# Two routers: half-tile logits behind the next half's products, ranking rounds between halves, and low halves behind the first gather

## The chip, the core and the metric

The kernel runs on one core of a Trainium2 chip. A core has five instruction queues that run in order and beside each other: TensorE (PE, matrix products into PSUM; its weight loads are listed as PEld), VectorE (DVE, elementwise work and searches), ScalarE (ACT, functions and copies), GpSimd (POOL, slow elementwise work and indirect DMAs) and SyncE (SP, which only starts DMAs here). They wait for each other by semaphores. The metric is the time of one execution on the device in microseconds, as the median of several runs.

## What is computed

Two layers of a diffusion backbone over 1024 latent and 256 context tokens of width 1024. Layer 0 mixes tokens with a bidirectional state-space scan (SSD), layer 1 with attention. After each mixer stands an expert-choice mixture of 16 experts: every expert picks its best tokens by a softmax over the experts.

```python
x = x + g1l * o_lat
x = x + g2l * moe_ec(rmsnorm(x, norm2_w[i]) * (1.0 + sc2l) + sh2l, ...)
...
def moe_ec(h, router_w, w1, w3, w2):
    logits = jnp.einsum('btd,de->bte', h, router_w)
    aff = jax.nn.softmax(logits, axis=-1)
    gate, idx = lax.top_k(jnp.swapaxes(aff, 1, 2), cap)   # cap = 2 * T // 16
    xg = h[bidx, idx]
    a = jnp.einsum('becd,edf->becf', xg, w1)
    g = jnp.einsum('becd,edf->becf', xg, w3)
    y = jnp.einsum('becf,efd->becd', jax.nn.silu(a) * g, w2)
    return jnp.zeros_like(h).at[bidx, idx].add(y * gate[..., None])
```

For 1024 latent tokens each expert takes 128, for 256 context tokens 32. Context tokens are only routed in layer 0.

## The kernel before

Tokens come in tiles of 128: ten in layer 0 (two of context, numbered 0 and 1, and eight of latents, 2 to 9, which go first), eight of latents in layer 1, numbered 0 to 7 here. Products in 32 bits are made of three passes: both operands are split into a high part (a copy by ScalarE, L48 and L722) and a low part (a subtraction on VectorE or GpSimd, L49, L723 and L725), and L54 to L56 multiply high by high, high by low and low by high.

**The output projection.** After each mixer a loop over tiles multiplies by the output weights, in two halves of 512 columns: 48 products a half in layer 0 (`ssd_out`, 16 blocks of rows in three passes), 24 in layer 1 (end of `attn`, 8 blocks). The products of a half are evaluated on VectorE: scaling by the gate (L626 in layer 0, L1254 in layer 1), adding the residual (L628, L1255), which gives `x1`. PSUM has two buffers for the first half (`o_ps0`) and one for the second.

**The router.** `Router.half` follows at once. It multiplies the half by a row of factors (L1341, into `u`, whose tiles are named h2), squares it on ScalarE with a sum (L1343), and `project` transposes the half on TensorE (L1318), copies it (L1320) and multiplies it by the router's weights into one PSUM bank (L1324). After the second half `Router.tile` makes the normalising factor (L1351, L159, L160), brings the logits into place (`logits`: L1329, L1331, L1332), writes them (L1355), finishes the normalised row (L1356) and starts two stores, the row to `h2` (L1359) and `x1` to `xs` (L1360), on SP, for the last tile on POOL.

**The ranking.** Tokens are ranked in parts: the first five latent tiles, the last three, and in layer 0 the two context tiles. `affinities` makes the softmax of a part and transposes it to one row per expert (L1368 to L1379). `rank` then finds the best 128 (32 for context) in rounds of eight, each with three searches on VectorE over the part's 640, 384 or 256 columns: MAX8 (L1390), FIND_INDEX8 (L1391), MATCH_REPLACE8 (L1393, not in the last round). `finish` merges the two latent rankings (L1403 to L1407), transposes the merged indices and gates on TensorE (L1409, L1410) and copies them (L1413, L1414). In layer 0 the ranking of the first part is called after the last latent tile and that of the second part ahead of the last context half's router; in layer 1 both are called after the loop.

**The first expert.** In `moe`, GpSimd gathers an expert's rows with an indirect DMA (L764); they are transposed and split, and `product` runs over four pieces of weights (`kp`), splitting each with GpSimd taking the last 128 (layer 0) or 256 (layer 1) of 1024 columns (L723) and VectorE the others (L725). In layer 1, GpSimd takes all columns of the first three pieces of the very first product. The split weights have three buffers.

**What sets the order.** The text is not the order in an engine's queue. A planner at compile time simulates the engines and gives each engine, when it comes free, the earliest instruction of the text that is ready, and one further down when that isn't. So an instruction can stand well before or behind its place in the text, and a place higher up in the text works as a priority. `issue_after(ins)` makes what is inside stand behind `ins` on that engine's queue, without waiting for its end.

Of the kernel before, what the change touches and what calls it, by code (L numbers as in the profile page):

```python
# [9 lines left out]
F32 = mybir.dt.float32  # L10
# [30 lines left out]
class Net:  # L41
# [534 lines left out]
    def ssd_out(self):  # L576
# [6 lines left out]
        with tc.tile_pool(name="op", bufs=2) as op:  # L583
# [3 lines left out]
            rt = Router(self, 0, op, pp, rk, [(NCT, NCT + 5), (NCT + 5, NT), (0, NCT)])  # L587
            for t in chain(range(NCT, NT), range(NCT)):
# [85 lines left out]
    def moe(self, i, ctx):  # L674
# [8 lines left out]
        with tc.tile_pool(name="mo", bufs=1) as mp, \  # L683
# [15 lines left out]
            def product(m, e, xl, xc, done=None):  # L699
# [16 lines left out]
                for kp in range(4):  # L716
                    n = D - (D if i and m + e == 0 and kp < 3 else share)
# [5 lines left out]
                    nc.gpsimd.tensor_tensor(w[1][:, :, n:], raw[:, :, n:], w[0][:, :, n:].bitcast(F32), op=OP.subtract)  # L723
                    if n:
                        nc.vector.tensor_tensor(w[1][:, :, :n], raw[:, :, :n], w[0][:, :, :n].bitcast(F32), op=OP.subtract)  # L725
# [150 lines left out]
            x = turn(gather(0))  # L876
# [82 lines left out]
    def attn(self):  # L959
# [273 lines left out]
        with tc.tile_pool(name="ao", bufs=2) as op:  # L1233
# [8 lines left out]
            rt.stream(0)  # L1242
            for t in range(NL):
                oh = self.hl_tile()
                self.split(q32[t].rearrange("p (j l) -> p j l", l=P), oh[0], oh[1], nc.gpsimd)
# [3 lines left out]
                for h in range(2):  # L1249
                    ps = pp.tile([P, 512], F32, name=f"o_ps{h}", bufs=2 - h)  # L1250
                    hs = slice(512 * h, 512 * h + 512)
                    for k in range(KT):
                        self.mm3(ps, [o[:, k] for o in oh], [w[:, k] for w in wo[h]], k == 0, k == KT - 1)
                    nc.vector.tensor_tensor(x1[:, hs], ps, gb[:, hs], op=OP.mult)  # L1254
                    nc.vector.tensor_tensor(x1[:, hs], x1[:, hs], xt[:, hs], op=OP.add)  # L1255
# [7 lines left out]
        first = rt.rank(0, af)  # L1263
# [21 lines left out]
class Router:  # L1285
# [48 lines left out]
    def half(self, x1, h):  # L1334

        nc, op = self.net.nc, self.op
# [9 lines left out]
    def tile(self, t, x1):  # L1346
# [10 lines left out]

        eng = nc.gpsimd if t + 1 == self.parts[-1][1] else nc.sync
        eng.dma_start(net.tile_of(net.h2d, t), self.u)  # L1359
        eng.dma_start(net.tile_of(net.xs, t), x1)  # L1360
# [21 lines left out]
    def rank(self, k, af, cap=CAPL):  # L1382

        net, nc, rp = self.net, self.net.nc, self.rk
        val = rp.tile([16, cap], F32, name=f"val{k}")
        idx = rp.tile([16, cap], U32, name=f"idx{k}")
        idf = rp.tile([16, cap], F32, name=f"idf{k}")
        for r8 in range(cap // 8):
            sl = slice(8 * r8, 8 * r8 + 8)
            nc.vector.max(val[:, sl], af)  # L1390
            nc.vector.max_index(idx[:, sl], val[:, sl], af)  # L1391
            if r8 + 1 < cap // 8:
# [76 lines left out]
```

## Time and profile before

| | us |
|---|---|
| median of three runs (3915.23 to 3926.81) | 3923.66 |
| the profiled execution, as timed | 3926.47 |
| its span, first to last instruction | 3924.7 |
| layer 0: output projection and router, to the first gathered rows | 1248 to 1530 |
| layer 0: experts | 1530 to 2360 |
| layer 1: attention | 2360 to 3083 |
| layer 1: output projection and router, to the first gathered rows | 3083 to 3286 |
| layer 1: experts and output | 3286 to 3924 |

The page of the profile gives busy time of each engine and the span in 40 slices of 98 us, busy shares in tenths:

```profile
PE 3570.0 (91%) x21153; PEld 2686.2 (68%) x21153; DVE 2620.5 (67%) x3749; ACT 2027.9 (52%) x3325; POOL 1814.0 (46%) x1402
...
PE   5999999888899997999999998899999874999997
...
DVE  4767777666633466666666655556656477999988
```

Slices 13 to 16 (1177 to 1570 us) hold layer 0's projection and slices 32 to 34 (3042 to 3336 us) layer 1's; the 4 in TensorE's row is the slice from 3238 to 3336. Other views used below are the waits (which engine waited for whom, us in total, number, longest), the timeline (start, duration, engine, line, operation, tiles, and in brackets the idle time before it and who ended it), the groups by line (count, busy us, mean ns) and busy time in stretches of the span.

### The profile page before, as it was taken

Reading aid. Unit: us, or ns where it says so; the run is one execution under the profiler, and the core shown is the slowest. Engines: PE = TensorE matmul, PEld = TensorE weight load, DVE = VectorE, ACT = ScalarE, POOL = GpSimd, SP = SyncE. Lnnn points to the kernel's source line nnn. Section 1 sums busy time; section 2 is a strip of 40 time slices with the busy share of each in tenths; the row PEclk is TensorE's granted clock in tenths of the full one; section 3 lists DMA queues with packets and bytes.
Section 4 is the critical chain, followed back from the end, with each engine's and each line's share of the span. In section 5 each row is a group of like instructions: output and inputs, shape, how many; then the busy total and the mean of one; then the engine's idle time right before and its main releaser. Section 6 shows DMA issues by size and latency. Waiting matters only on the chain.

```text
span 3924.7 us, 56652 instructions
## 1 busy us (share of the span) xinstructions
PE 3570.0 (91%) x21153; PEld 2686.2 (68%) x21153; DVE 2620.5 (67%) x3749; ACT 2027.9 (52%) x3325; POOL 1814.0 (46%) x1402
## 2 busy tenths in 40 slices
PE   5999999888899997999999998899999874999997
PEld 3767677777787775667666767677777653777765
DVE  4767777666633466666666655556656477999988
ACT  4544444544333223545555545477777433777665
POOL 1356545554543223566666652221111123777786
PEclk7999999999999998999999999999999987999999
DMA  4333332222444335889888863100000345999994
GB/s 171 103 103 127 115 96 77 76 76 74 143 142 144 126 115 183 325 313 330 313 319 307 285 236 92 38 15 1 1 1 12 129 142 212 386 376 376 350 338 172
DMA packets 296355, 681.08 MB, mean 174 GB/s; under 512 B 24192, under 2 KB 150000, under 8 KB 289936
## 3 DMA queue, kind: packets, MB, share of 16 engines
q1 hardware_dynamic: 269520, 615.50, 43.7%
q0 software_dynamic: 12720, 39.33, 4.1%
q10 hardware_dynamic: 13840, 22.63, 1.8%
q8 instruction: 167, 2.74, 0.3%
q14 instruction: 108, 0.88, 0.1%
HBM read 611.95 MB, written 62.82 MB: 172 GB/s over the span
## 4 chain that ended last, share of the span: by engine, by line
PE 54%; DVE 17%; POOL 9%; issue 9%; DMA 7%; ACT 4%; ACTq 0%; SPq 0%; POOLq 0%; DVEq 0%
DVE m_w L725 6%; PE pv L1171 5%; PE acc L54 4%; PE acc L56 4%; PE acc L55 4%; PE S L1137 4%; PE a_tr L1158 4%; PE cacc L696 4%; POOL m_w L723 3%; PE in_ps L55 3%; PE in_ps L54 3%; PE in_ps L56 3%; POOL Eb L422 2%; DMA m_raw<-in_moe_w_dram 2%; DMA Eb<-fd 2%
## 5 line engine op out<-in xcount | busy, mean ns | idle before, releaser
L725 DVE TENSOR_TENSOR m_w<-m_raw,m_w 128x1792 fp32r<-128x1792 f32 (+1 forms) x381 | 887.9, 2352 | 249.3 <-ACT m_w L722 247.1
L723 POOL TENSOR_TENSOR m_w<-m_raw,m_w 128x256 fp32r<-128x256 f32 (+1 forms) x384 | 816.1, 2149 | 387.9 <-ACT m_w L722 385.0
L722 ACT ACTIVATE m_w<-m_raw 128x2048 fp32r<-128x2048 f32 x384 | 732.8, 1916 | 483.2 <-DMA m_raw<-in_moe_w_dram 276.9
L54 PE MATMUL in_ps<-hh,w 128*128 128x512 f32 (+1 forms) x1152 | 427.6, 371 | 10.3 <-DVE th L499 10.3
L55 PE MATMUL acc<-m_w,xl 128*128 128x512 f32 x1024 | 406.9, 397 | 23.3 <-DVE m_w L725 12.5
L55 PE MATMUL in_ps<-hl,w 128*128 128x512 f32 (+1 forms) x1152 | 427.3, 371 | 0.0
L56 PE MATMUL in_ps<-hh,w 128*128 128x512 f32 (+1 forms) x1152 | 425.5, 369 | 0.0
L54 PE MATMUL acc<-m_w,xl 128*128 128x512 f32 x1024 | 405.6, 402 | 2.0 <-ACT xl L48 1.9
L56 PE MATMUL acc<-m_w,xl 128*128 128x512 f32 x1024 | 401.3, 392 | 0.0
L427 ACT ACTIVATE Eb<-Eb,ebias 128x128 f32<-128x128 f32 x640 | 202.2, 391 | 249.7 <-POOL Eb L422 249.5
L1141 DVE TENSOR_REDUCE mx<-S 128x1 f32<-128x1024 f32 x128 | 155.7, 1217 | 185.0 <-PE S L1137 184.9
L54 PEld LDWEIGHTS in_ps<-hh,w 128*128 128x128 f32 x1152 | 222.8, 193 | 52.8 <-issue 14.3
L55 PEld LDWEIGHTS acc<-m_w,xl 128*128 128x128 f32 x1024 | 193.2, 189 | 82.9 <-DVE m_w L725 26.9
L55 PEld LDWEIGHTS in_ps<-hl,w 128*128 128x128 f32 x1152 | 222.9, 193 | 39.1 <-issue 13.5
L1188 POOL TENSOR_TENSOR q<-s 64x128 f32<-64x128 f32 x128 | 57.5, 449 | 407.3 <-DVE mx L1146 339.5
L56 PEld LDWEIGHTS in_ps<-hh,w 128*128 128x128 f32 x1152 | 222.6, 193 | 31.7 <-issue 5.5
L54 PEld LDWEIGHTS acc<-m_w,xl 128*128 128x128 f32 x1024 | 193.0, 189 | 67.1 <-issue 14.4
L328 POOL TENSOR_TENSOR w<-w_raw,w 128x512 fp32r<-128x512 f32 x96 | 149.9, 1581 | 186.6 <-ACT w L325 181.3
L56 PEld LDWEIGHTS acc<-m_w,xl 128*128 128x128 f32 x1024 | 193.5, 189 | 38.1 <-DVE xl L49 0.2
L55 PE MATMUL acc<-m_w,gT 128*128 128x512 f32 x512 | 204.1, 399 | 6.6 <-DVE m_w L725 4.0
L54 PE MATMUL acc<-m_w,gT 128*128 128x512 f32 x512 | 202.2, 401 | 1.5 <-ACT gT L48 1.5
L56 PE MATMUL acc<-m_w,gT 128*128 128x512 f32 x512 | 202.3, 396 | 0.1
(385 smaller groups left out, 7724.7 us busy)
## 6 DMA issues: line engine op xcount, KB each, us to landing
m_raw<-in_moe_w_dram SPq DMA_DIRECT2D x384, 1024.0 KB
adw<-in_ada_w_dram SPq DMA_DIRECT2D x48, 1024.0 KB
Eb<-fd SPq DMA_DIRECT2D x80, 512.0 KB
w_raw<-in_ssd_in_w_dram SPq DMA_DIRECT2D x48, 512.0 KB
ydd<-yd SPq DMA_DIRECT2D x80, 128.0 KB
yt_raw<-yzd SPq DMA_DIRECT2D x40, 256.0 KB
xs<-x SPq DMA_DIRECT2D x16, 512.0 KB
h<-h SPq DMA_DIRECT2D x16, 512.0 KB
```

The source lines that it names most:

```text
L54: mm(out, lhs[0], rhs[0], start=start, stop=False)
L55: mm(out, lhs[0], rhs[1], start=False, stop=False)
L56: mm(out, lhs[1], rhs[0], start=False, stop=stop)
L427: nc.scalar.activation(Eb[:, d, hh, cc], Eb[:, d, hh, cc], AF.Exp, bias=bias[:, c0 + cc, k:k + 1])
L696: nc.tensor.matmul(acc[32 * q:32 * q + 32], xc[:, k], raw[:, k % 2, 256 * q:256 * q + 256], start=(k == 0), stop=(k == KT - 1))
L722: nc.scalar.activation(w[0], raw, AF.Copy)
L723: nc.gpsimd.tensor_tensor(w[1][:, :, n:], raw[:, :, n:], w[0][:, :, n:].bitcast(F32), op=OP.subtract)
L725: nc.vector.tensor_tensor(w[1][:, :, :n], raw[:, :, :n], w[0][:, :, :n].bitcast(F32), op=OP.subtract)
L1137: nc.tensor.matmul(o, qTs[self.qt][:, 2 * self.hp + hh], kT[k][:, self.kv, 512 * b:512 * b + n], start=(k == 0), stop=(k == 1))
L1141: nc.vector.tensor_reduce(self.mx[:, 0:1], S[hh], axis=AX.X, op=OP.max)
L1158: nc.tensor.transpose(ps[:, q], self.pr[hh][:, (c0 + q) * P:(c0 + q + 1) * P], net.ident)
L1171: nc.tensor.matmul(self.pv[o:o + 64, 0], v32[:, t, self.kv], self.PT[:, t], start=(t < 2), stop=(t >= NT - 2))
```

## The change

1. **Logits a half later.** `Router.half` no longer projects. A new `close` projects the half that was evaluated last and, after a second half, calls `tile`. Both loops call it after the next half's products, and once after the loop. The `x1` store moves from `tile` into `half`.
2. **Rounds between halves.** A ranking is now an object (`Rank`) whose `go(n)` issues n more rounds. In layer 0 the first part's ranking starts when tile 6 is closed, with three rounds after each following half; the second part's when tile 9 is closed, with six rounds. In layer 1 the first part's ranking starts when the fifth tile is closed, with three rounds a half; the second part's comes after the loop as before.
3. **The merge of layer 0** stands before the last context half's products in place of behind them.
4. **Low halves.** GpSimd's low halves of the first expert's first product stand behind the first gather (`issue_after`), and layer 1's first three pieces are shared between GpSimd and VectorE like all others. In layer 1's projection the low halves of the attention output (L49 into `hl`) go from GpSimd to VectorE.

```diff
@@ ssd_out
+            before = first = second = None
             for t in chain(range(NCT, NT), range(NCT)):
...
                 for h in range(2):
+                    if t + 1 == NCT and h == 1:
+                        rt.finish(first, second)
                     for k in range(16):
                         self.mm3(...)
...
+                    if before is not None:
+                        rt.close(before)
+                        if h == 0 and before + 1 == NCT + 5:
+                            first = rt.rank(0, rt.affinities(0))
+                        if h == 0 and before + 1 == NT:
+                            second = rt.rank(1, rt.affinities(1))
+                    before = t
...
-                    if t + 1 == NCT and h == 1:
-                        rt.finish(first, rt.rank(1, af1))
-                    rt.half(x1, h)
-                rt.tile(t, x1)
-                if t + 1 == NCT + 5:
-                    af = rt.affinities(0)
-                if t + 1 == NT:
-                    af1 = rt.affinities(1)
-                    first = rt.rank(0, af)
+                    rt.half(t, x1, h)
+                    if second:
+                        second.go(6)
+                    elif first:
+                        first.go(3)
+            rt.close(before)
             self.ctx_rank = rt.rank(2, rt.affinities(2), CAPC)
+            self.ctx_rank.all()
@@ product
-                    n = D - (D if i and m + e == 0 and kp < 3 else share)
+                    n = D - share
...
-                    nc.gpsimd.tensor_tensor(w[1][:, :, n:], raw[:, :, n:], ...)
-                    if n:
-                        nc.vector.tensor_tensor(w[1][:, :, :n], raw[:, :, :n], ...)
+                    with tc.issue_after(self.gathered.ins) if m + e == 0 else nullcontext():
+                        nc.gpsimd.tensor_tensor(w[1][:, :, n:], raw[:, :, n:], ...)
+                    nc.vector.tensor_tensor(w[1][:, :, :n], raw[:, :, :n], ...)
@@ moe
-            x = turn(gather(0))
+            x = gather(0)
+            self.gathered = self.fetched
+            x = turn(x)
@@ attn
+            before = first = None
             for t in range(NL):
                 oh = self.hl_tile()
-                self.split(q32[t]..., oh[0], oh[1], nc.gpsimd)
+                self.split(q32[t]..., oh[0], oh[1], nc.vector)
...
+                    if before is not None:
+                        rt.close(before)
+                        if h == 0 and t == 5:
+                            first = rt.rank(0, rt.affinities(0))
+                    before = t + NCT
...
-                    rt.half(x1, h)
-                rt.tile(t + NCT, x1)
-                if t == 4:
-                    af = rt.affinities(0)
+                    rt.half(t + NCT, x1, h)
+                    if first:
+                        first.go(3)
+            rt.close(before)
...
-        first = rt.rank(0, af)
         rt.finish(first, rt.rank(1, rt.affinities(1)))
@@ Router
-    def half(self, x1, h):
+    def half(self, t, x1, h):
...
+        self.open = (x1, h)
+        if h:
+            self.store(t).dma_start(net.tile_of(net.xs, t), x1)
+
+    def store(self, t):
+        return self.net.nc.gpsimd if t + 1 == self.parts[-1][1] else self.net.nc.sync
+
+    def close(self, t):
+        h = self.open[1]
         self.project(self.u, h)
+        if h:
+            self.tile(t)
...
-        eng.dma_start(net.tile_of(net.h2d, t), self.u)
-        eng.dma_start(net.tile_of(net.xs, t), x1)
+        self.store(t).dma_start(net.tile_of(net.h2d, t), self.u)
@@ rank
+class Rank:
+    def go(self, n):
+        for r8 in range(self.r8, min(self.r8 + n, self.cap // 8)):
+            sl = slice(8 * r8, 8 * r8 + 8)
+            nc.vector.max(self.val[:, sl], self.af)
+            nc.vector.max_index(self.idx[:, sl], self.val[:, sl], self.af)
+            if r8 + 1 < self.cap // 8:
+                nc.vector.match_replace(self.af, self.val[:, sl], self.af, -1.0)
+            self.r8 = r8 + 1
+    def all(self):
+        if self.done:
+            return self.val, self.idf
+        self.go(self.cap // 8)
+        ...
```

More of the change, by code (lines that the diff above doesn't have):

```diff
@@ L1 @@
 import math
-from contextlib import ExitStack
+from contextlib import ExitStack, nullcontext
 from itertools import chain
@@ L722, in product @@
                     nc.scalar.activation(w[0], raw, AF.Copy)
-                    nc.gpsimd.tensor_tensor(w[1][:, :, n:], raw[:, :, n:], w[0][:, :, n:].bitcast(F32), op=OP.subtract)
-                    if n:
-                        nc.vector.tensor_tensor(w[1][:, :, :n], raw[:, :, :n], w[0][:, :, :n].bitcast(F32), op=OP.subtract)
+                    with tc.issue_after(self.gathered.ins) if m + e == 0 else nullcontext():
+                        nc.gpsimd.tensor_tensor(w[1][:, :, n:], raw[:, :, n:], w[0][:, :, n:].bitcast(F32),
+                                                op=OP.subtract)
+                    nc.vector.tensor_tensor(w[1][:, :, :n], raw[:, :, :n], w[0][:, :, :n].bitcast(F32), op=OP.subtract)
                     for kk in range(2):
@@ L1242, in attn @@
             rt.stream(0)
+            before = first = None
             for t in range(NL):
                 oh = self.hl_tile()
-                self.split(q32[t].rearrange("p (j l) -> p j l", l=P), oh[0], oh[1], nc.gpsimd)
+                self.split(q32[t].rearrange("p (j l) -> p j l", l=P), oh[0], oh[1], nc.vector)
                 xt = op.tile([P, D], F32, name="xt")
@@ L1332, in logits @@
         nc.vector.tensor_reduce(dst, lt[:, :, 0:E].rearrange("p q e -> p e q"), axis=AX.X, op=OP.add)
-    def half(self, x1, h):
-        nc, op = self.net.nc, self.op
+    def half(self, t, x1, h):
+        net, nc, op = self.net, self.net.nc, self.op
         if h == 0:
@@ L1343, in half, with tile @@
         nc.scalar.activation(sq.rearrange("p q l -> p (q l)"), x1[:, hs], AF.Square, accum_out=self.ss[:, h:h + 1])
+        self.open = (x1, h)
[5 more added lines that the diff above has]
+        h = self.open[1]
         self.project(self.u, h)
-    def tile(self, t, x1):
+        if h:
+            self.tile(t)
+    def tile(self, t):
         net, nc, op = self.net, self.net.nc, self.op
@@ L1382, in rank @@
     def rank(self, k, af, cap=CAPL):
[L1384 to L1392, printed above, removed]
-                nc.vector.match_replace(af, val[:, sl], af, -1.0)
-        nc.vector.tensor_scalar(idf, idx, float(max(self.parts[k][0] - NCT, 0) * P), None, op0=OP.add)
-        return val, idf
+        return Rank(self, k, af, cap)
     def finish(self, first, second):
         net, nc, pp, rp = self.net, self.net.nc, self.pp, self.net.rtp
-        v, i = first
-        v2, i2 = (t[:, ::-1] for t in second)
+        v, i = first.all()
+        v2, i2 = (t[:, ::-1] for t in second.all())
         m = self.rk.tile([16, CAPL], F32, name="m_ge")
@@ L1419, in finish_ctx @@
         ps = pp.tile([P, 2, E], F32, name=self.tag or "r_lg", bufs=2 if self.tag else 1)
-        for k, v in enumerate(first):
+        for k, v in enumerate(first.all()):
             v4 = self.rk.tile([16, 4, CAPC], F32, name="v4")
@@ L1432, in finish_ctx, with __init__ @@
         nc.vector.tensor_scalar(net.idxC4, ps[:, 1], 4.0, blk, op0=OP.mult, op1=OP.add)
+class Rank:
+    def __init__(self, rt, k, af, cap):
+        self.rt, self.k, self.af, self.cap, self.r8 = rt, k, af, cap, 0
+        self.done = False
+        self.val = rt.rk.tile([16, cap], F32, name=f"val{k}")
+        self.idx = rt.rk.tile([16, cap], U32, name=f"idx{k}")
+        self.idf = rt.rk.tile([16, cap], F32, name=f"idf{k}")
+    def go(self, n):
+        nc = self.rt.net.nc
+        for r8 in range(self.r8, min(self.r8 + n, self.cap // 8)):
[9 more added lines that the diff above has]
+        self.go(self.cap // 8)
+        self.done = True
+        self.rt.net.nc.vector.tensor_scalar(self.idf, self.idx, float(max(self.rt.parts[self.k][0] - NCT, 0) * P), None,
+                                            op0=OP.add)
+        return self.val, self.idf
 _INS = ["x", "c", "ctx", "c_ctx", "ada_w", "ada_b", "norm1_w", "norm2_w", "ssd_in_w", "ssd_conv_w", "ssd_conv_b",
```

1 line of the change is left out of this document (removed).

## The prediction

> **What bounds the kernel now.** I read the page's slices first, then, for the two places that the change touches, TensorE's waits, then busy time by stretch, then the timelines. TensorE is busy nearly throughout, and the change can only win where it is not: the two output projections with the routers behind them, 3083 to 3289 us (layer 1) and 1248 to 1533 (layer 0). TensorE's waits in 3108 to 3290, then in 1290 to 1532, then ScalarE's longest in 3289 to the end (line, what it waited for, us, times, longest):
>
> ```profile
> PE r_lg L1409 <- DVE idf L1407: 39.9, 1, 39.9
> PE r_tr L1318 <- DVE h L1341: 11.7, 4, 7.1
> PE r_tr L1318 <- DVE ss L1351: 5.8, 3, 2.1
> ...
> PE r_tr L1318 <- DVE h L1341: 5.4, 6, 2.3
> ...
> ACT m_w L722 <- PE acc L56: 90.1, 90, 3.0
> ```
>
> In layer 1 TensorE waits for VectorE: 17.5 us at L1318, the router's transposition of the half tile that was just evaluated, and 39.9 us at the end, where the ranking runs. Layer 0 loses only 5.4 us at L1318. Busy time by stretch (PE, PEld, DVE, ACT, POOL, granted clock):
>
> ```profile
> 3112.00:3172.00 60.00, 51.95 (x270) 37.40 (x270) 31.02 (x43) 17.72 (x37) 10.49 (x4) 0.94 0.46 173
> 3172.00:3217.00 45.00, 41.81 (x224) 30.97 (x222) 37.77 (x72) 15.61 (x39) 4.87 (x2) 0.96 0.34 117
> 3217.00:3289.00 72.00, 6.32 (x28) 3.99 (x29) 63.24 (x147) 10.50 (x17) 16.40 (x7) 0.53 0.44 160
> ```
>
> Up to 3172 nobody is saturated, so the order is at fault; from 3217 VectorE does nearly everything, so its total work counts. What follows the first gather is the experts. There the weights' high halves (L722) wait for TensorE to give buffers back, not for the weights, so a shift of the gather passes through to the end.
>
> **The change, layer 1: logits after the next half's products.** Evaluation of tile 3's and tile 4's halves (L1254; the product before it has just ended), then L1341's durations (least, median, most, ns) and the two stretches after tile 2's last product (granted clock in the third column from the end):
>
> ```profile
> 3148.24 0.69 DVE L1254 TENSOR_TENSOR x<-o_ps,g1b 128x512 f32<-128x512 f32 x1 [0.43 <-PE o_ps L56]
> 3154.91 0.69 DVE L1254 TENSOR_TENSOR x<-o_ps,g1b 128x512 f32<-128x512 f32 x1 [4.53 <-PE o_ps L56]
> 3165.33 0.69 DVE L1254 TENSOR_TENSOR x<-o_ps,g1b 128x512 f32<-128x512 f32 x1 [0.42 <-PE o_ps L56]
> ...
> L1341 DVE TENSOR_TENSOR h<-x,a x36: 658/691/4315, 1290.9 to 3219.6; 128x512 f32<-128x512 f32 x36
> ...
> 3139.00:3142.00 3.00, 1.00 (x5) 0.49 (x3) 2.97 (x3) 0.72 (x2) 2.45 (x1) 1.00 0.66 187
> 3142.00:3146.00 4.00, 3.94 (x12) 2.86 (x12) 1.52 (x4) 0.78 (x2) 0.00 (x0) 0.57 0.31 126
> ```
>
> A half without a stall takes 3154.91 - 3148.24 = 6.67 us, one with it 10.42: the stall costs 3.75: about 1.9 of waiting (5.8 in three) and the rest in products at a clock of 0.57. Put the close behind the next half's 24 products and the evaluation (L1254, L1255 and L1341, of one shape: 0.69 each, some 2.1) is covered by 6.67 us. So I forecast 6.67 for every half once the weights are there:
>
> ```profile
> 3112.11 0.69 DVE L1254 TENSOR_TENSOR x<-o_ps,g1b 128x512 f32<-128x512 f32 x1 [0.23 <-PE o_ps L56]
> 3182.41 0.69 DVE L1254 TENSOR_TENSOR x<-o_ps,g1b 128x512 f32<-128x512 f32 x1 [0.43 <-PE o_ps L56]
> 3181.49 0.23 DVE L1332 TENSOR_REDUCE r_lr<-r_lg 128x16 f32<-128x64 f32 x1 [1.99 <-PE r_lg L1331]
> 3188.30 0.81 DVE L1390 MAX8 val<-af 16x8 f32<-16x640 f32 x1
> ...
> 1463.02 0.75 DVE L626 SCALAR_TENSOR_TENSOR x<-o_ps,yr,g1b 128x512 f32<-128x512 f32 x1 [9.08 <-PE o_ps L56]
> 1470.11 0.23 DVE L1332 TENSOR_REDUCE r_lr<-r_lg 128x16 f32<-128x64 f32 x1 [0.81 <-PE r_lg L1331]
> ```
>
> From tile 1's first half (3112.11) to tile 5's first half are eight halves: 53.4 us, so 3165.5 in place of 3182.41. The delay has its price here: tile 4's logits, which the first ranking needs, now come after tile 5's first half. In layer 0's last latent tile (last two rows) the logits come 7.1 us after the product's end, some 3 of it the evaluation, which is now done before: 4. That gives 3169.5 against 3181.49, so the first ranking starts 12.0 us earlier, at 3176.3 instead of 3188.30. Bounds: 7 if the waiting goes but three times 1.8 at the low clock stays, 16.9 if the planner puts the close earlier.
>
> **Layer 1: VectorE from the first ranking to the gather.** Groups of VectorE in 3188.2 to 3281.7 (count | busy, mean ns of one):
>
> ```profile
> L1390 DVE MAX8 val<-af 16x8 f32<-16x640 f32 x16 | 12.9, 807 | 0.2
> L1391 DVE FIND_INDEX8 idx<-val,af 16x8 uint32<-16x640 f32 x16 | 12.9, 806 | 0.0
> ...
> L1356 DVE SCALAR_TENSOR_TENSOR h<-h,rstd,s 128x1024 f32<-128x1024 f32 x3 | 8.3, 2776 | 0.0
> ...
> L1341 DVE TENSOR_TENSOR h<-x,a 128x512 f32<-128x512 f32 x5 | 7.0, 1394 | 0.0
> L1255 DVE TENSOR_TENSOR x<-x,xt 128x512 f32<-128x512 f32 x5 | 4.8, 964 | 0.0
> ...
> 3120.14 1.28 DVE L1356 SCALAR_TENSOR_TENSOR h<-h,rstd,s 128x1024 f32<-128x1024 f32 x1
> 3218.84 4.51 POOL L723 TENSOR_TENSOR m_w<-m_raw,m_w 128x2048 fp32r<-128x2048 f32 x1 [26.80 <-ACT m_w L722]
> ```
>
> Rounds already lie between the halves here: the planner takes them whenever VectorE's next instruction is not ready. So "rounds between halves" moves little; I cost it at nothing, between 4 us won (more rounds of the two rankings paired) and 4 lost (evaluations behind rounds, VectorE idle in the last tile's logits). What does go is contention: L1356, L1341 and L1255 with GpSimd beside them take 8.3 + 7.0 + 4.8 = 20.1 us, at 1.28 and 0.69 each they would take 3 x 1.28 + 10 x 0.69 = 10.7. With GpSimd's splits on VectorE and its low halves behind the gather, 9.4 us go. Added, from these prices:
>
> ```profile
> L49 DVE TENSOR_TENSOR hl<-xt,hl x10: 1210/1220/1226, 2361.2 to 2502.9; 128x1024 fp32r<-128x1024 f32 x10
> 1547.34 2.02 DVE L725 TENSOR_TENSOR m_w<-m_raw,m_w 128x1792 fp32r<-128x1792 f32 x1 [5.94 <-ACT m_w L722]
> ```
>
> One query split of 1.22 (the price is that of the same shape in the attention; the other splits come earlier, under products), and three low halves of 1536 columns, 2.02 x 1536 / 1792 = 1.73 each: 5.2. They could hide in the 4 us in which the gather lands, but their inputs are ready long before, so I put them on the path; bounds 0 and 5.2. Sum for layer 1: -12.0 - 9.4 + 1.2 + 5.2 = -15.0, and I take -14, with 1 us for an idle VectorE at the last tile. Ends: -20 (the low halves hidden) and -5 (a start 7 earlier, rounds in the way by 4, a second split).
>
> **The added wait.** GpSimd's four low halves of the first product now queue behind the first gather, the next gather behind them, and TensorE waits for both. By L723's 4.51 us for 2048 columns, 512 take 1.1. The first two gathers:
>
> ```profile
> 3281.76 1.01 POOL L764 DMA_INDIRECT xg<-h,idxL  x1 [46.81 <-DVE at L832]
> 3288.30 0.97 POOL L764 DMA_INDIRECT xg<-h,idxL  x1 [5.54 <-PE m_tr L760]
> ```
>
> From one to the next are 6.5 us, 5.54 of it a wait for TensorE, so three of them fit: nothing. In layer 0 they stand behind the gather already. The x1 stores move ahead of the h2 stores on SP and POOL and go early; the h2 stores go half a tile later, and the buffer (two in layer 1) is wanted a whole tile later: nothing.
>
> **Layer 0.** Evaluations of tile 5's second half and of tile 6's halves, then the stage's end and the two merges (L1403):
>
> ```profile
> 1363.21 0.75 DVE L626 SCALAR_TENSOR_TENSOR x<-o_ps,yr,g1b 128x512 f32<-128x512 f32 x1 [9.79 <-PE o_ps L56]
> 1376.38 0.75 DVE L626 SCALAR_TENSOR_TENSOR x<-o_ps,yr,g1b 128x512 f32<-128x512 f32 x1 [6.07 <-PE o_ps L56]
> 1388.35 0.75 DVE L626 SCALAR_TENSOR_TENSOR x<-o_ps,yr,g1b 128x512 f32<-128x512 f32 x1 [9.77 <-PE o_ps L56]
> ...
> 1475.12 1.23 DVE L1307 SCALAR_TENSOR_TENSOR a<-a,h 128x1024 f32<-128x1024 f32 x1 [4.28 <-DMA h<-h]
> 1478.23 0.55 DVE L1390 MAX8 val<-af 16x8 f32<-16x384 f32 x1
> 1519.52 0.75 DVE L626 SCALAR_TENSOR_TENSOR x<-o_ps,yr,g1b 128x512 f32<-128x512 f32 x1 [2.96 <-PE o_ps L56]
> 1525.35 1.01 POOL L764 DMA_INDIRECT xg<-h,idxL  x1 [0.56 <-issue]
> 1541.62 0.80 PE L55 MATMUL acc<-m_w,xl 128*128 128x512 f32 x1 [4.17 <-POOL m_w L723]
> ...
> L1403 DVE TENSOR_TENSOR m_ge<-val,val x2: 260/260/260, 1515.1 to 3278.8; 16x128 f32<-16x128 f32 x2
> ```
>
> A first half takes 13.17, a second 11.97: 1.2 of stall in each of four or five tiles, so the last latent half moves 5 us up, from 1463.02 to 1458. But the last latent tile's logits now wait for 12.0 us of the first context half: L1332 at 1458 + 12.0 + 4 = 1474, and the second ranking starts 4 to 8 us behind it (1478.23 - 1470.11 = 8.1 now, of which 4.28 is L1307's wait), 1478 to 1482: no earlier than today. It lasts 36.9 us, to 1515 to 1519. Now the merge of 1515.1 lies until the gather of 1525.35, because its result is transposed after the last half's logits; after, it stands before them. In layer 1, where nothing is in its way, the gather follows the merge by 3281.76 - 3278.8 = 3.0 us: 1518 to 1522, a gain of 3 to 7, and I take 5. The last half, four halves behind 1458, ends near 1507 in place of 1519.5, so it does not hold the gather. The 4.17 us stall goes if the low halves precede the gathered rows; half of it: 2. Sum -7, ends -12 and +2.
>
> **The rivals.** First, **contention moves into the first expert**: the low halves meet L725 and the splits of the gathered rows just when TensorE needs them, and the 4.17 us stall stays in layer 0 and appears in layer 1. For it: that row. Against: four times less GpSimd work in layer 1. It costs 2 + 4.2: gain 15, 3909. The Trainium skill, in "SBUF — State Buffer", section "Who interferes with whom", states that a VectorE instruction with two SBUF inputs and a GpSimd instruction reading SBUF exclude each other for the whole instruction; the trace agrees (L1341 takes 4315 ns beside the L723 of 4.51 us, 691 in the median). By that rule the gain would be this rival's 15 wherever L723 and L725 meet.
>
> Second, **evaluations stand behind three rounds** on VectorE in layer 1: a round is three searches of 0.8, so three are 7.2 us, more than the 6.67 us half. Then the last evaluation comes after 15 rounds and VectorE idles while its logits form: layer 1 wins 5, layer 0 5, 3914. Against: the interleaving above.
>
> Third, on the other side, **TensorE keeps the text's order at the merge** in layer 0: L1409 before the last half's 48 products. They would be ready at 1458 + 38 = 1496 and wait for the ranking's end, 1517 to 1521; then 12 us and 1.7 for a low clock, 1531 to 1535 against 1519.5: 14 late for all that follows. With the second rival's layer 1 and the first's stall there, 14 - 5 + 4 = 13 slower: 3937. It decides as soon as L1409 precedes any of those products. Against: the planner hoists what is ready.
>
> Fourth, more: paired rounds, low halves under the gather, layer 0 at its end: gain 31, 3893.
>
> **How the numbers follow.** -14 - 7 = -21. The profiled execution took 3926.47 (span 3924.7), 2.8 above the median of 3923.66; 3905.5 there is 3902.7 as a median: 3903. If its layer ends both fall short (-5 and +2), it would be 3921. Chances: forecast 0.58, first 0.15, second 0.12, third 0.07, fourth 0.08. The range takes in the fourth's end and the second's, with the bounds of layer 1: 3890 to 3918. A measurement here tells about 0.3% (11.8 us) from no change. Faster by more: 0.56 + 0.11 + 0.03 + 0.08 = 0.78; within: 0.17; slower: 0.05.
>
> **What would show it.** Layer 1's halves at 6.7 us without clock dips; L1318's waits gone; MAX8 of the first ranking 11 to 17 us after tile 5's first half's product ends; L1356 at 1.28; the gather near 3268 less layer 0's 7. In layer 0, L1409 ahead of the last half's logits and the gather near 1520. I am wrong if halves stay at 10.4, if L1409 blocks products, or if PE waits for L723 after the gather.

## The result, and the profile after

The changed kernel takes 3897.79 us (median of five runs, 3887.77 to 3902.36) against 3923.66 before (3915.23 to 3926.81): 25.9 us less, a ratio of 0.9935 with a 95% interval of 0.9914 to 0.9956. The forecast was 3903. The profiled execution took 3890.86 us (span 3889.1), 35.6 less than the profiled one of before, 10 more than the medians differ by; where part of those 10 lies is taken up below.

To compare stages, five instants are read from each timeline: **P**, the first product of layer 0's output projection; **G0**, layer 0's first gather; **T**, layer 1's first evaluation of tile 1 (its first half); **M**, layer 1's first MAX8; **G1**, layer 1's first gather. Busy time by stretch, before (length, busy us of PE, PEld, DVE, ACT, POOL with counts, granted clock, DMA share, GB/s); the rows are P to G0, T to M, M to G1, G1 to the end:

```profile
1248.81:1525.35 276.54, 257.31 (x1278) 195.18 (x1278) 159.18 (x315) 76.00 (x157) 58.50 (x43) 0.98 0.42 141
3112.11:3188.30 76.19, 66.14 (x335) 48.11 (x336) 40.55 (x59) 24.02 (x56) 12.95 (x5) 0.93 0.42 157
3188.30:3281.76 93.46, 30.95 (x177) 21.90 (x175) 90.48 (x200) 18.60 (x34) 17.12 (x7) 0.67 0.44 157
3281.76:3924.70 642.94, 586.06 (x2592) 456.48 (x2592) 578.27 (x349) 425.76 (x316) 486.68 (x224) 0.98 0.89 327
```

The same four stretches of the changed kernel:

```profile
1247.45:1517.00 269.55, 254.22 (x1277) 196.64 (x1277) 155.86 (x313) 76.28 (x155) 57.90 (x43) 0.97 0.43 145
3097.49:3161.70 64.21, 63.46 (x351) 48.41 (x352) 36.89 (x68) 25.28 (x57) 0.00 (x0) 1.00 0.52 190
3161.70:3244.86 83.16, 27.18 (x161) 19.03 (x159) 80.28 (x199) 17.41 (x33) 1.23 (x2) 0.66 0.35 133
3244.86:3889.10 644.24, 586.13 (x2592) 456.88 (x2592) 580.86 (x351) 425.60 (x316) 492.29 (x227) 0.98 0.90 331
```

Layer 0's projection is 7.0 us shorter, layer 1's up to the ranking 12.0, its ranking 10.3, and 1.3 are given back behind the gather: 28.0 in all (7.0 + 12.0 + 10.3 - 1.3). The rest of the 35.6 lies ahead of P (1.4) and between G0 and T (6.3), in layer 0's experts and the attention, where two executions of one order differ by 4.3 (below).

The forecast's instants, T, tile 5's first half and M, in VectorE's timeline:

```profile
3097.49 0.69 DVE L1272 TENSOR_TENSOR x<-o_ps,g1b 128x512 f32<-128x512 f32 x1 [0.22 <-PE o_ps L56]
...
3150.98 0.69 DVE L1272 TENSOR_TENSOR x<-o_ps,g1b 128x512 f32<-128x512 f32 x1 [2.76 <-PE o_ps L56]
...
3161.70 0.82 DVE L1464 MAX8 val<-af 16x8 f32<-16x640 f32 x1
```

Eight halves take 53.5 us, 6.7 each. In T to M, GpSimd's column has gone from 12.95 us to none, and TensorE is busy for 63.46 of 64.21 us at full clock where it had 66.14 of 76.19 at 0.93. TensorE's waits in layer 1 after the change, 3097 to 3260 us (line, what it waited for, us, times, longest):

```profile
PE r_lg L1425 <- DVE idf L1423: 41.8, 1, 41.8
PE r_tr L1405 <- DVE lg L1399: 7.8, 1, 7.8
...
PE r_tr L1335 <- DVE h L1358: 2.8, 2, 2.0
```

The 17.5 us of waits at the transposition (now L1335) have shrunk to 2.8; the wait for the ranking stays, 41.8, because VectorE is at work almost without a gap until G1 (80.28 of 83.16 us). VectorE's groups in that stretch (count | busy, mean ns):

```profile
L1386 DVE SCALAR_TENSOR_TENSOR h<-h,rstd,s 128x1024 f32<-128x1024 f32 x3 | 3.8, 1254 | 0.0
L735 DVE TENSOR_TENSOR m_w<-m_raw,m_w 128x1536 fp32r<-128x1536 f32 x2 | 3.5, 1740 | 0.0
L1358 DVE TENSOR_TENSOR h<-x,a 128x512 f32<-128x512 f32 x4 | 2.7, 669 | 0.0
...
L1273 DVE TENSOR_TENSOR x<-x,xt 128x512 f32<-128x512 f32 x4 | 2.6, 659 | 0.0
```

The normalised rows take 1.254 us where they took 2.776, and four halves are evaluated here, not five: tile 5's second half is now evaluated ahead of M (at 3157.57), while the affinities form. Of the three low halves that VectorE took over, one stands inside the ranking and two begin as the gather is issued (timeline of VectorE and GpSimd):

```profile
3189.99 1.73 DVE L735 TENSOR_TENSOR m_w<-m_raw,m_w 128x1536 fp32r<-128x1536 f32 x1
...
3244.18 3.42 DVE L735 TENSOR_TENSOR m_w<-m_raw,m_w 128x1536 fp32r<-128x1536 f32 x2
...
3244.86 1.94 POOL L774 DMA_INDIRECT xg<-h,idxL  x1 [47.77 <-DVE gL L1430]
```

Layer 0 after the change: last latent half, its logits, second ranking, last context half, merge, gather, context's gather:

```profile
1456.72 0.75 DVE L636 SCALAR_TENSOR_TENSOR x<-o_ps,yr,g1b 128x512 f32<-128x512 f32 x1 [0.75 <-PE o_ps L56]
1471.44 0.23 DVE L1349 TENSOR_REDUCE r_lr<-r_lg 128x16 f32<-128x64 f32 x1
1477.37 0.55 DVE L1464 MAX8 val<-af 16x8 f32<-16x384 f32 x1
...
1509.51 0.72 DVE L636 SCALAR_TENSOR_TENSOR x<-o_ps,yr,g1b 128x512 f32<-128x512 f32 x1
1512.88 0.26 DVE L1419 TENSOR_TENSOR m_ge<-val,val 16x128 f32<-16x128 f32 x1
...
1517.00 1.01 POOL L774 DMA_INDIRECT xg<-h,idxL  x1 [0.35 <-issue]
...
1540.85 0.88 POOL L774 DMA_INDIRECT xgc<-h,idxC  x1 [1.22 <-DVE idxC L1448]
```

The products end earlier (1509.5 against 1519.5), the second ranking starts where it did, and the gather follows the merge by 4.1 us instead of 10.2. TensorE's products for the last half's logits (L1324, now L1341) and its transposition of the merged indices (L1409, now L1425), first before, then after:

```profile
1523.18 0.43 PE L1324 MATMUL r_lg<-h2T,rw 128*32 128x128 f32 x8 [0.75 <-ACT h2T L1320]
1524.01 0.23 PE L1409 MATMUL r_lg<-ident,idf 16*128 16x16 f32 x1 [0.40 <-ACT r_ls L1329]
...
1514.45 0.25 PE L1425 MATMUL r_lg<-ident,idf 16*128 16x16 f32 x1 [1.30 <-DVE rstd L160]
...
1516.08 1.08 PE L1341 MATMUL r_lg<-h2T,rw 128*32 128x128 f32 x16 [1.27 <-DVE gL L1430]
```

Before, the transposition stood behind the logits of the last half; after, it stands ahead of them, as the prediction said it would.

### The profile page after: what moved, and what is told of

It is laid out like the page before. It is cut to its first block, busy times and chain, and to the rows that moved or that the text cites. A ratio compares the mean times of both kernels' runs of the same rounds, so it can differ in the third digit from the quotient of the medians.

```text
span 3889.1 us, 56643 instructions
## 1 busy us (share of the span) xinstructions
PE 3556.7 (91%) x21153; PEld 2683.1 (69%) x21153; DVE 2602.3 (67%) x3760; ACT 2028.4 (52%) x3325; POOL 1785.3 (46%) x1394
## 4 chain that ended last, share of the span: by engine, by line
PE 38%; DVE 10%; issue 6%; POOL 4%; DMA 4%; ACT 2%; SPq 0%; ACTq 0%; POOLq 0%; DVEq 0%
DVE m_w L735 6%; PE pv L1183 5%; PE acc L54 4%; PE acc L56 4%; PE acc L55 4%; PE S L1149 4%; PE a_tr L1170 4%; PE cacc L704 4%; POOL m_w L733 3%; DMA m_raw<-in_moe_w_dram 2%; PE o_ps L55 1%; PE o_ps L56 1%; PE o_ps L54 1%; PE qkv L56 1%; PE qkv L54 1%
## 5 line engine op out<-in xcount | busy, mean ns | idle before, releaser
L735 DVE TENSOR_TENSOR m_w<-m_raw,m_w 128x1792 fp32r<-128x1792 f32 (+1 forms) x384 | 889.2, 2338 | 242.9 <-ACT m_w L730 241.6
L733 POOL TENSOR_TENSOR m_w<-m_raw,m_w 128x256 fp32r<-128x256 f32 (+1 forms) x384 | 807.0, 2114 | 351.1 <-ACT m_w L730 349.5
L54 PE MATMUL in_ps<-hh,w 128*128 128x512 f32 (+1 forms) x1152 | 428.2, 372 | 10.2 <-DVE th L499 10.2
```

The costliest lines, as they stand in the source:

```text
L54: mm(out, lhs[0], rhs[0], start=start, stop=False)
```

## The experiments

The stages of all kernels, each from the timeline of its one profile (us; T to end is to the end of the span), and the ratio of its runs to runs of the kernel before on the same chip:

| kernel | P to G0 | T to M | M to G1 | G1 to end | T to end | ratio (95%) |
|---|---|---|---|---|---|---|
| before | 276.5 | 76.2 | 93.5 | 642.9 | 812.6 | |
| changed | 269.5 | 64.2 | 83.2 | 644.2 | 791.6 | 0.9935 (0.9914 to 0.9956) |
| merge behind | 268.8 | 64.2 | 83.2 | 644.3 | 791.7 | 0.9943 (0.9924 to 0.9962) |
| ranking whole | 268.1 | 64.2 | 83.2 | 644.3 | 791.7 | 0.9941 (0.9925 to 0.9958) |
| logits at once | 273.0 | 61.9 | 86.3 | 646.3 | 794.5 | 0.9957 (0.9940 to 0.9974) |
| GpSimd as before | 268.6 | 67.5 | 91.0 | 642.8 | 801.3 | 0.9963 (0.9948 to 0.9978) |
| before + query split | 276.8 | 60.3 | 93.1 | 643.8 | 797.2 | 0.9953 (0.9934 to 0.9972) |
| before + part 4 | 275.5 | 60.3 | 86.9 | 644.6 | 791.8 | 0.9942 (0.9914 to 0.9970) |
| + part 4, layer 0 deferred | 269.7 | 60.4 | 87.0 | 644.3 | 791.7 | 0.9935 (0.9911 to 0.9958) |
| changed, layer 1 at once | 268.7 | 60.3 | 86.9 | 644.8 | 792.0 | 0.9935 (0.9915 to 0.9956) |
| changed, no order | 269.1 | 64.2 | 86.4 | 646.0 | 796.6 | 0.9928 (0.9906 to 0.9950) |
| last latent at once | 260.9 | 64.2 | 83.2 | 644.6 | 792.0 | 0.9918 (0.9888 to 0.9948) |
| low halves behind merge | 268.2 | 64.2 | 81.9 | 646.9 | 793.0 | 0.9919 (0.9893 to 0.9946) |

The intervals overlap nearly everywhere, so the verdicts below rest on the stages, which repeat to a few tenths in layer 1's projection and ranking.

**Is it the order of the logits?** First, logits at once again in both loops, all else as changed:

```diff
-                    if before is not None:
-                        rt.close(before)
...
                     rt.half(t + NCT, x1, h)
+                    rt.close(t + NCT)
...
```

> The changed kernel, but every half's logits are formed at once again (the close stands right behind the half's evaluation, in both layers); rankings, rounds and GpSimd's share stay as changed. Theory A, the order of the logits is worth what the traces suggest: in layer 1 the eight halves from tile 1's first to tile 5's first take 69 to 71 us again instead of 53.5 and the first ranking starts 12 us later against tile 1's first half; in layer 0 the last half's products end some 10 us later and the gather comes at 1523 to 1527 instead of 1517.0, although the second ranking can start some 3 us earlier; in all 17 to 25 us slower than the changed kernel (3897.8): 3915 to 3923. Theory B, the gain came from GpSimd's work leaving VectorE alone and from the placing of the rounds: halves go back to 10.4 us but the gather of layer 1 moves by less than 5 and the time stays at 3898 to 3905.

Neither theory as written held. Layer 0's gather came at 1523.43, in theory A's range, but P too came 3.0 us later in this execution, so layer 0 lost 3.5 us. In layer 1 the halves did **not** go back to 10.4 us: they stayed at 6.67, and M came 2.3 us earlier after T than in the changed kernel. So the stall was gone with the logits in their old order. VectorE in one of these halves, in the kernel with the logits at once:

```profile
3138.72 0.69 DVE L1264 TENSOR_TENSOR x<-o_ps,g1b 128x512 f32<-128x512 f32 x1 [4.53 <-PE o_ps L56]
3139.44 0.69 DVE L1265 TENSOR_TENSOR x<-x,xt 128x512 f32<-128x512 f32 x1
3140.05 1.22 DVE L49 TENSOR_TENSOR hl<-q,hl 128x1024 fp32r<-128x1024 f32 x1
3141.18 0.68 DVE L1352 TENSOR_TENSOR h<-x,a 128x512 f32<-128x512 f32 x1
...
3145.38 0.69 DVE L1264 TENSOR_TENSOR x<-o_ps,g1b 128x512 f32<-128x512 f32 x1 [0.20 <-PE o_ps L56]
```

And the same place in the kernel before, VectorE, GpSimd and TensorE:

```profile
3139.22 2.78 DVE L1341 TENSOR_TENSOR h<-x,a 128x512 f32<-128x512 f32 x1
...
3138.97 2.49 POOL L49 TENSOR_TENSOR hl<-q,hl 128x1024 fp32r<-128x1024 f32 x1 [13.08 <-ACT hl L48]
...
3142.06 0.74 PE L1318 MATMUL r_tr<-ident,h 128*128 128x128 f32 x4 [2.06 <-DVE ss L1351]
```

Before, GpSimd's split of the attention output lies across the evaluation's last step: 2.78 us where it takes 0.68, and the missing 2.1 us are TensorE's wait of 2.06 (the view names L1351, the short reduction right behind L1341). On VectorE the split costs 1.22 us and lengthens nothing else. The logits' order makes no wait here once GpSimd's work is gone. The test of that is the kernel before with this one edit:

```diff
-                self.split(q32[t]..., oh[0], oh[1], nc.gpsimd)
+                self.split(q32[t]..., oh[0], oh[1], nc.vector)
```

> The kernel before with a single edit: the split of the attention output into hl on VectorE instead of GpSimd. Theory A: L1341 at 0.7 us in place of 2.78 in the second halves, no waits of TensorE at L1318, no clock at 0.57; 62 to 65 us instead of 76.2 from tile 1's first half to the first MAX8; from there to the gather 91 to 95 as before, because the low halves of the weights still run on GpSimd; 10 to 14 us below the kernel before. Theory B, the 1.22 us that VectorE now has in front of the evaluation's last step stand in for the 2.1 us that go, and the stall only shrinks from 2.06 to about 1.2: 68 to 73 us and at most 5 below.

Theory A, and more than its size. Its stretches T to M and M to G1 (cut 0.03 us behind M), the first with TensorE at full clock for 59.61 of 60.36 us:

```profile
3105.54:3165.90 60.36, 59.61 (x331) 44.30 (x332) 35.52 (x64) 24.57 (x56) 0.00 (x0) 1.00 0.54 199
3165.90:3258.93 93.03, 31.72 (x181) 22.59 (x179) 89.44 (x201) 18.82 (x34) 14.68 (x5) 0.66 0.43 158
```

One word wins 15.4 of the 21.0 us that the whole change wins from T to the end. What it leaves is the weights' low halves on GpSimd during the ranking (14.68 us in the second row). All of part 4 in the kernel before:

> The kernel before with part 4 alone: the query split of layer 1 on VectorE, the first three pieces shared, GpSimd's low halves behind the first gather; logits at once, rankings as before. Theory A, the stall of layer 1 came from GpSimd's query split beside the evaluation and not from the order of the logits: halves at 6.67 us, 62 to 64 us instead of 76.2 from tile 1's first half to the first MAX8, 84 to 88 instead of 93.5 from there to the gather, and layer 0's stage as before (276.5 from its first product to the gather): 16 to 20 us below the kernel before, ratio 0.995 to 0.996. Theory B, the deferral is needed as well: halves of 10.4 us remain, at most 10 us are won.

Theory A again, a little beyond its sizes: T to end 791.8, as in the changed kernel (791.6). Its diff is part 4 of the change. M to G1 falls from 93.1 to 86.9, and the rest of the way to 83.2 is only moved: M lies 3.9 us earlier after T than in the changed kernel, because tile 4's logits needn't wait for tile 5's products.

**Then what is the deferral worth in layer 1?** Two runs. GpSimd's part as before in the changed kernel:

```diff
-                    n = D - share
+                    n = D - (D if i and m + e == 0 and kp < 3 else share)
...
-                    with tc.issue_after(self.gathered.ins) if m + e == 0 else nullcontext():
...
-                self.split(q32[t]..., oh[0], oh[1], nc.vector)
+                self.split(q32[t]..., oh[0], oh[1], nc.gpsimd)
```

> The changed kernel, but GpSimd's part is as before: in layer 1 it takes the low halves of the first three weight pieces whole, not bound to stand behind the gather, and the low halves of the attention output. Theory A, contention: the three L1386-like instructions take about 2.8 us again instead of 1.26 and the evaluations 1.0 to 1.4 instead of 0.67; the stretch from the first MAX8 to layer 1's gather grows from 83.2 to 89 to 92 us; the time is 6 to 9 us above the changed kernel: 3904 to 3907. Theory B, the contention lay where VectorE had slack, or is offset by the low halves that VectorE no longer has to make: within 2 us of the changed kernel, 3896 to 3900.

T to M is 67.5, M to G1 91.0:

```profile
3098.42:3165.91 67.49, 62.90 (x346) 47.68 (x347) 43.31 (x62) 24.99 (x57) 15.52 (x6) 1.00 0.54 193
3165.91:3256.95 91.04, 29.61 (x166) 20.71 (x164) 86.56 (x197) 17.61 (x33) 14.96 (x5) 0.65 0.40 150
```

GpSimd's 15.52 us are back and TensorE's clock stays at 1.00: the deferral does cover the slow evaluation, but for 3.3 us ahead of M. Theory A's 89 to 92 for M to G1 is met, though only in part by the instructions that it named. L1386 kept 1.26 us; one evaluation step (L1273, 4.27 us beside a GpSimd split of 4.51) and one step of the logits took the load:

```profile
L1273 DVE TENSOR_TENSOR x<-x,xt 128x512 f32<-128x512 f32 x4 | 6.3, 1564 | 0.0
L1385 DVE SCALAR_TENSOR_TENSOR lg<-r_lr,rstd,r_c 128x16 f32<-128x16 f32 x3 | 4.9, 1623 | 0.0
```

In the changed kernel their means are 0.66 and 0.21. T to end is 9.7 worse than changed, and 11.3 better than before. So **each of the two removes the stall by itself**, and together they win nothing more, as layer 1's old loop in the changed kernel shows:

```diff
-                    if before is not None:
-                        rt.close(before)
-                        if h == 0 and t == 5:
-                            first = rt.rank(0, rt.affinities(0))
...
+                    rt.close(t + NCT)
+                if t == 4:
+                    af = rt.affinities(0)
...
```

> The changed kernel, but with layer 1's loop as in the kernel before: logits at once, both rankings called after the loop; layer 0 and GpSimd's part stay as changed. Theory A, in layer 1 the deferral and the placing of the rounds add nothing once GpSimd's part is changed: 790 to 793 us from tile 1's first half to the end (791.6 in the changed kernel, 791.8 with part 4 alone), the time that of the changed kernel. Theory B, they add what the prediction gave them, some 12 us: 800 and more.

792.0 against 791.6: theory A. Splitting the rounds between the halves is worth nothing either:

```diff
-                        second.go(6)
+                        second.go(16)
...
-                        first.go(3)
+                        first.go(16)
...
```

> The changed kernel, but each ranking issues its 16 rounds at once at its place in the text instead of three or six behind each half. Theory A, the planner interleaves rounds and evaluations by itself: landmarks of layer 1 (first MAX8 to gather, 83.2 us) and the gather of layer 0 (1517.0) move by under 2 us, time 3898 within 5. Theory B, the placing counts: rounds stand ahead of evaluations, TensorE waits for evaluations in the middle of the ranking and the last tile's logits come later than 3193; the stretch from the first MAX8 to the gather grows by 5 to 10 us, and layer 0's last half ends later: 3905 to 3915.

64.2, 83.2 and 791.7 are the changed kernel's numbers to 0.1 us: theory A. That holds with the logits deferred. With the logits at once, calling layer 1's first ranking early and in threes cost 2.5 us (T to end 794.5, against 792.0 with both rankings called after the loop); why stays open.

**The order behind the gather.** Without it:

```diff
-                    with tc.issue_after(self.gathered.ins) if m + e == 0 else nullcontext():
+                    with nullcontext():
```

> The changed kernel without the order that puts GpSimd's low halves of the first product behind the first gather; the shares stay (256 of 1024 columns on GpSimd). Theory A, they then run during layer 1's ranking, each beside VectorE for 1.1 to 2.5 us, three of them: from the first MAX8 to the gather 85 to 88 us instead of 83.2, and the gather's own issue at about 1.0 us; 2 to 4 above the changed kernel. Theory B, VectorE loses nothing: 83.2, and the first product, whose halves are then ready, starts as early: equal to the changed kernel.

M to G1 grew to 86.4 as theory A said, and T to end by 5.0, more than its 2 to 4; the 1.8 of it behind the gather stay open. Only part of M to G1's 3.2 is contention: all three of VectorE's low halves now stand inside the ranking (groups, M to G1):

```profile
L735 DVE TENSOR_TENSOR m_w<-m_raw,m_w 128x1536 fp32r<-128x1536 f32 x3 | 5.2, 1728 | 0.0
...
L1273 DVE TENSOR_TENSOR x<-x,xt 128x512 f32<-128x512 f32 x4 | 3.1, 764 | 0.0
```

The opposite, none of them inside, by an order for VectorE's as well:

```diff
-                    nc.vector.tensor_tensor(w[1][:, :, :n], ...)
+                    with tc.issue_after(self.merged.ins) if m + e == 0 else nullcontext():
+                        nc.vector.tensor_tensor(w[1][:, :, :n], ...)
...
-        nc.vector.tensor_copy(net.gL, ps[:, 1])
+        net.merged = nc.vector.tensor_copy(net.gL, ps[:, 1])
```

> The changed kernel, but VectorE's low halves of the first product stand behind the merge's last copy, so that none of them lies in layer 1's ranking (one of 1.73 us does in the changed kernel, and two run beside the gather's issue, which takes 1.94 us there). Theory A, the ranking is VectorE's work without a gap, so that all of the 1.73 comes back: 81.3 to 81.7 us from the first MAX8 to the gather instead of 83.2, and the first product no later behind the gather: 790 us instead of 791.6 from tile 1's first half to the end. Theory B, three low halves in a row beside GpSimd's delay the gathered rows' splits, and what the ranking gains goes there: 81.5, and 791.5 to 793.

Theory B: M to G1 falls to 81.9, but behind the gather the three meet GpSimd's three and take longer, and the end comes 2.7 later after G1 (groups of instructions in VectorE's and GpSimd's timelines):

```profile
3250.58 6.15 DVE L736 TENSOR_TENSOR m_w<-m_raw,m_w 128x1536 fp32r<-128x1536 f32 x3
...
3253.27 5.82 POOL L733 TENSOR_TENSOR m_w<-m_raw,m_w 128x512 fp32r<-128x512 f32 x3
```

**Layer 0: the merge, the deferral, or the rankings' place?** The merge called behind the last half's products:

```diff
                 for h in range(2):
-                    if t + 1 == NCT and h == 1:
-                        rt.finish(first, second)
...
+                    if t + 1 == NCT and h == 1:
+                        rt.finish(first, second)
                     if before is not None:
```

> The changed kernel, but layer 0's merge is called behind the last context half's products again instead of ahead of them. Theory A, the step of the prediction that gave the merge's place 3 to 7 us: the gather of layer 0 comes at 1520 to 1524 instead of 1517.0, the time is 5 above the changed kernel, 3903. Theory B, the place in the text changes nothing, because the merge's instructions become ready after the last product in either case and no engine's queue comes out in another order: the gather at 1517 within 0.5, and what differs from 3897.8 is what two measurements of one order differ by.

Theory B; every engine has its work in the order of the changed kernel, and G0 follows P by 268.8. (G0 itself came at 1520.8, in theory A's range, but P too came 4.5 us later.) This run is also a measure of chance: one order, and yet P comes at 1252.0 instead of 1247.5, layer 0's experts take 834.7 us from G0 instead of 830.5 (to the first split of the attention), and G0 to T takes 1584.8 instead of 1580.5. Next, the deferral in layer 0 alone, on top of part 4, with the merge behind the products and both rankings called as late as in the kernel before:

```diff
...
+                    if before is not None:
+                        rt.close(before)
+                        if h == 0 and before + 1 == NCT + 5:
+                            af = rt.affinities(0)
+                        if h == 0 and before + 1 == NT:
+                            af1 = rt.affinities(1)
+                            first = rt.rank(0, af)
+                    before = t
+                    if t + 1 == NCT and h == 1:
+                        rt.finish(first, rt.rank(1, af1))
...
```

> The kernel before with part 4 and, in layer 0 alone, the deferred logits; the rankings of layer 0 are called where the kernel before calls them (the first part's after the last latent tile, the second's with the merge behind the last half's products), and layer 1's logits are formed at once. Theory A, in layer 0 the deferral brings the gain: from the projection's first product to the gather 268 to 271 us, as in the changed kernel, against 275.5 with part 4 alone. Theory B, the earlier place of the rankings brings it, since with logits at once and the new places it was 273.0: 273 to 276. In layer 1 the same as with part 4 alone: 791 to 793 us from tile 1's first half to the end. Total: A 4 to 7 below, B within 2 of part 4 alone.

Theory A: 269.7, so in layer 0 the deferral brings it by itself (the new places by themselves, with the logits at once, brought 2.5 of the 275.5 with part 4 alone, to 273.0):

```profile
1247.28:1517.00 269.72, 254.63 (x1278) 195.87 (x1278) 157.76 (x315) 77.78 (x157) 57.30 (x43) 0.97 0.43 145
```

With 3890.87 us (before on that chip: 3919.45) this kernel, which has neither rounds between halves nor a deferral in layer 1, is as fast as the changed one. The 4 to 7 us that theory A set for the total against part 4 alone can't be told from the ratios (0.9935 and 0.9942, on two chips). Last, the deferral taken away only where the second ranking waits for it:

```diff
-                        if h == 0 and before + 1 == NT:
-                            second = rt.rank(1, rt.affinities(1))
...
                     rt.half(t, x1, h)
+                    if h and t + 1 == NT:
+                        rt.close(t)
+                        before = None
+                        second = rt.rank(1, rt.affinities(1))
```

> The changed kernel, but in layer 0 the last latent tile's second half is closed at once, so that the second ranking needn't wait for the first context half's products; the rest is deferred as changed. Theory A, the second ranking sets layer 0's gather: it starts some 8 us earlier, and from the projection's first product to the gather are 261 to 264 us instead of 268.1 to 269.6; 4 to 8 below the changed kernel. Theory B, the last half's products and their evaluation set it (1509.5 in the changed kernel's profile, and three to six us behind them): 265 to 268, and 2 below the changed kernel at most, which the time can't tell.

G0 did come 8 us earlier, 260.9 after P, but that won nothing. GpSimd's first gather and the context's in this kernel:

```profile
1511.32 1.15 POOL L776 DMA_INDIRECT xg<-h,idxL  x1 [22.05 <-DMA m_raw<-in_moe_w_dram]
...
1543.60 0.91 POOL L776 DMA_INDIRECT xgc<-h,idxC  x1 [1.21 <-DVE idxC L1450]
```

The context's gather stands 293.2 us behind P (1250.4), in the changed kernel 293.4 (1540.85 - 1247.45), and layer 0 ends 1102.4 behind P against 1099.5 to 1103.9 in the kernels with the changed layer 0 (1107.6 to 1112.4 in the three with that of before). The latents' gather had stopped being what layer 0's end waits for. That the context's gather is what it waits for now is argued from this; no run moved that gather alone, and one row speaks against it: with the logits at once the context's gather comes 4.1 us later against P (297.5), and layer 0 still ends at 1101.9.

## Why the prediction was right in its time, and where it was not

**Layer 1's stall: the size held, the cause didn't.** The step said "so the order is at fault" and gave the deferral 12.0 us. T to M fell by 12.0, tile 5's first half came 53.5 us behind T (forecast 53.4), and the ranking 10.7 behind that. But the stall was GpSimd's split of the attention output beside L1341. With that split left on GpSimd, the deferral won 8.7 of the 12.0 (T to M 67.5); without it, the deferral costs 3.9 (64.2 against 60.3). The prediction had the evidence in a row it quoted, GpSimd busy for 2.45 of the 3 us at 3139, and L1341's range of 658 to 4315 ns, and used neither for this wait. The Trainium skill, in "SBUF — State Buffer", section "Who interferes with whom", says that a VectorE instruction with two SBUF inputs and a GpSimd instruction that reads SBUF exclude each other; the trace agrees (2.78 us beside a split of 2.49, 0.68 without it).

**Rounds between halves: nothing.** Right, to 0.1 us in layer 1, where the logits are deferred.

**Contention during the ranking: 9.4 us.** Right in price: 1.254 and 0.66 to 0.67 us an instruction against the 1.28 and 0.69 that were put in. Part 4 alone, which takes GpSimd out of the ranking, brought M to G1 from 93.5 to 86.9 with one low half of 1.73 us in it.

**Added work: 5.2 + 1.2 us put on the path, 1.73 found there.** This is the term that was mis-sized. The query split lies in T to M, under products; two of the three low halves lie behind the gather's indices, where VectorE would wait for rows. The prediction named that place and chose the other bound. It also left out that one half's evaluation, 3 x 0.67 = 2.0, moves out of the ranking. With the 1.3 given back behind the gather (below), layer 1 won 21.0 instead of 14, a little past the end of -20 that stood for hidden low halves.

**The added wait: nothing.** It costs nothing (GpSimd makes the three low halves of layer 1 and still stands idle for 1.43 us, waiting for TensorE, ahead of the second gather), but the order that makes it is worth 5.0 us: without it all of VectorE's low halves go into the ranking.

**Layer 0: -7 forecast, -7.0 in P to G0 (-7.0 to -8.4 in the seven kernels with that layer 0), by another way.** The second ranking started no earlier, as said (229.4 and 229.9 us behind P). The 5 us for the gather were given to the merge's place in the text; that place changes no order. The merge's transposition did come to stand ahead of the last half's logits, but by the deferral: the last half ends 8.6 us earlier against P (1519.52 - 1248.81 = 270.7 and 1509.51 - 1247.45 = 262.1), so that TensorE is free when the merge is done. The 2 us for the stall of 4.17 were no gain of the change. The same wait in the kernel before with the query split moved, whose layer 0 is the one of before, and in the changed kernel:

```profile
PE acc L55 <- POOL m_w L723: 0.4, 1, 0.4
...
PE acc L55 <- POOL m_w L733: 1.7, 1, 1.7
```

So most of the 4.17 us belonged to that one execution of before, and with them probably a few of the microseconds by which the two profiles differ more than the medians. And the wait that the prediction named as a sign of being wrong, TensorE waiting for GpSimd's low half after the gather, is there in the changed layer 0: 1.7 us (1.4 to 1.7 in five of the six other kernels with that layer 0, none in the sixth) against 0.3 to 0.4 with that of before. That the forecast and the result are both -7 is therefore in part luck.

**The rivals.** Contention in the first expert is there, but small: behind the gather 1.3 us were lost in layer 1 (642.9 to 644.2), not 4.2, and the wait in layer 0 is 1.7. Evaluations behind rounds did not happen. TensorE did not keep the merge's text order: no product stood behind it. The fourth rival's "low halves under the gather" is what came in layer 1.

## What to carry to other kernels

When TensorE waits for a vector instruction, first compare that instruction's duration with its own median, and look at what GpSimd does in the same microseconds: a wait that looks like a matter of order can be a neighbour's load, and moving one split can do the work of a reordered loop. Two edits that each remove the same stall don't add, so price each with the other already made. Compare stages between landmarks, not spans: two executions of one order differed by 4.5 us before the changed code began.

## What the runs showed of the hardware that was not expected

GpSimd's issue of layer 1's first gather took longer in the kernels in which VectorE subtracts two SBUF operands at that time: 1.94 us in the changed kernel, beside the L735 shown above (1.84 to 1.95 in all nine of them), and 1.01 us in the four without one, as in the kernel without the order:

```profile
3246.36 1.01 POOL L774 DMA_INDIRECT xg<-h,idxL  x1 [50.67 <-DVE at L842]
```

That would account for 0.9 of the 1.3 us that layer 1 gives back behind its gather; no run had the gather issued alone in an otherwise unchanged order.
